# Two chunks of the state-space recurrence per visit, norm sums as columns, one operand for two running sums

## The chip, the core and the metric

The kernel runs on one core of one Trainium2 chip. The engines that matter are PE (TensorE, the matmuls), DVE (VectorE), ACT (ScalarE), POOL (GpSimd, which does elementwise work here) and SP (SyncE, which issues most DMAs). Each engine takes its own instructions strictly in the order in which they stand in its queue, and semaphores order the engines among each other. The metric is the device time of one execution in microseconds (us); lower is better.

## What is computed

One decoder layer over 1024 tokens of width 1024, all in float32. One projection of the normalized input gives all branches; a state-space branch (Mamba-2, chunked) and an attention branch with a forget gate are gated, merged, projected and normalized. The part that the change touches:

```python
dt = softplus(dt_raw + dt_bias);  a = -exp(a_log)
da_cs = cumsum(dt * a)                       # within each chunk of 128 tokens, per head
decay = exp(where(causal, da_cs[l] - da_cs[s], -inf))
y_diag = (C B^T * decay) @ (xs * dt)         # within the chunk
states = B^T @ (xs * dt * exp(da_cs[-1] - da_cs))
# over the chunks, one after the other:
carry = carry * exp(da_cs[-1]) + states
y_off = (C @ carry_before) * exp(da_cs)
y = y_diag + y_off + xs * d_skip
# gated group norm: 4 groups of 256 channels
yg = y * silu(z_ssm);  yg = yg * rsqrt(mean(yg * yg) + eps) * g
# attention: F = cumsum(log_sigmoid(f)) over all tokens, per head
```

There are 16 heads of 64 channels in 4 groups; a group shares B and C (128 states).

## The kernel before

**The stream.** All large products go through PE as one long list of steps. A step is one of the seven products of a fast matrix multiplication for a pair of weight columns; it is 12 matmuls of 128 x 512 (each operand is split into a high and a low part), in two halves of six. `Stream.half()` issues the next half. The other work of the kernel is written as generators: `stream.beside(gen)` runs a piece of such a generator and then as many halves as it yields. On PE everything stands in program order (`mm`, `turn`), so PE's order is what this weaving makes of it. ACT and DVE prepare the weights of the steps ahead (tiles `wop`, `sum`) and take the results out of PSUM (`s`, `th`, `u`). On ACT, DVE and POOL only the instructions in `pin` keep program order among themselves; the others are put where a scheduler finds a place by its own estimate of time, and `tc.high_priority()` moves an instruction ahead of others that could start. Once built, the order on each engine is fixed.

**The recurrence.** `ssd(g)` does one group of four heads, chunk by chunk (8 chunks of 128 tokens). Of a chunk there are:
- `sums(c)`: a DMA by SP that spreads the running sums of the chunk over all partitions (tile `csb`, three chunks ahead);
- `decays(c)`: on ACT four Relu and one Exp make the decay matrix `m4`;
- `first(c)`: on PE the turns (transposes) of two value tiles and of B, and the product of B and C (all into PSUM tile `tr`); DVE makes `xdt` and `cbm` from them and multiplies `m4` by `cbm`; ACT copies the turned B to `bn`;
- `more(c)`: on POOL `xe` (the weighted values for the state), on ACT `ce = Exp(csb)`, on POOL `ce` times C;
- `second(c)`: on PE the state product (`st`), on POOL the old state times its decay (`new`), on DVE that plus `st`; on PE the outputs into `yps`, first `m4` by `xdt` (within the chunk), then `ce` by the state before (carried in); after each second chunk DVE adds the skip path.

One visit of a chunk issues `first(c + 1)`, then `second(c)`, then `more(c + 1)`; four halves of the stream lie between one visit and the next. So the state that `second(c)` makes is used one visit later, and what `first` and `more` prepare is used one visit later.

**Norm sums.** `squares(g, ch, ...)` adds the squares of 256 channels per token: the squares are split in a high and a low part (ACT, DVE), two matmuls of 128 x 512 against a matrix of ones give the sums in all rows (`pv`), ACT copies one row, and four one-row turns make columns of it (`pv_t`).

**Running sums.** `dt_and_f()` makes `dtn` (dt and log f side by side) and `da = -dt * a`; three products of `da` (`pt_te`) give the sums after a token, of the chunk and up to a token, as columns; four products per half of the tokens give the sums as rows (`pt_cs`), and four more those of log f (`pt_f`).

Buffers of the pool `sp`: `csb` 2, `ce` 1, `xe` 1, `bn` 1, `m4` 2, `xdt` 2.

Of the kernel before, what the change touches and what calls it, by code (L numbers as in the profile page):

```python
# [86 lines left out]
def hybrid_layer(ctx: ExitStack, tc, a, out):  # L87
# [596 lines left out]
    def dt_and_f():  # L684

        def rows(tag, bufs):
            t = sp.tile([P, 4, P], F32, tag=tag, bufs=bufs, name="rows")
            return t.rearrange("p a b -> p (a b)")[0:HEADS, :]

        pair = [  # L690
            sp.tile([P, 4, P], F32, tag="csb", bufs=2, name="t").rearrange("p a b -> p (a b)") for _ in range(2)
# [24 lines left out]
        for n in (13, 11, 9, 7, 5, 3, 1):  # L716
# [7 lines left out]
        nc.vector.scalar_tensor_tensor(  # L724
            dtn[:, :, 0:16], w[:, :, 0:16], 2.0, z2[:, :, 0:16], ALU.mult, ALU.add
        )
        nc.vector.scalar_tensor_tensor(
            dtn[:, :, 16:32], w[:, :, 16:32], -2.0, z2[:, :, 16:32], ALU.mult, ALU.add
        )

        nc.vector.scalar_tensor_tensor(
            da, dtn[:, :, 0:16], -1.0, ea.unsqueeze(1).to_broadcast([P, NT, HEADS]), ALU.mult, ALU.mult
        )
        yield 8

        daf = da.rearrange("p c h -> p (c h)")
# [4 lines left out]
        nc.scalar.activation(tend, pe_[:, 0:P].rearrange("p (c h) -> p c h", c=NT), AF.Exp)  # L741
        nc.scalar.activation(cdec, pe_[:, P : 2 * P].rearrange("p (c h) -> p c h", c=NT), AF.Exp)
        nc.scalar.activation(cscol, pe_[:, 2 * P : 3 * P].rearrange("p (c h) -> p c h", c=NT), AF.Copy)
# [10 lines left out]
        fc = [rows("ce", 1), rows("csb", 2)]  # L754
        for ch in range(2):
            pf = pp.tile([P, HALF], F32, tag="tr", bufs=2, name="pt_f")
            for j in range(4):
                c = ch * 4 + j
                mm(
                    pf[0:HEADS, j * P : (j + 1) * P], dtn[:, c, 16:32], tri, start=True, stop=True  # L760
                )
            for j in range(4):
                c = ch * 4 + j
                o, w = fc[ch][:, j * P : (j + 1) * P], pf[0:HEADS, j * P : (j + 1) * P]
# [76 lines left out]
    def ssd(g):  # L841
# [4 lines left out]
        def sums(c):  # L846

            if c < NT:
                csb = at[c]["csb"] = sp.tile([P, 4, P], F32, tag="csb", bufs=2, name="csb")
                nc.sync.dma_start(csb, cs_dram[hs, c * P : (c + 1) * P].unsqueeze(0).to_broadcast([P, 4, P]))  # L850

        def first(c):
# [16 lines left out]
            if c < NT - 1:  # L869
                bn = s["bn"] = sp.tile([P, P], F32, tag="bn", bufs=1, name="bn")  # L870
# [17 lines left out]
        def more(c):  # L888
# [3 lines left out]
            if c < NT - 1:  # L892
                xe = s["xe"] = sp.tile([P, 4, 64], F32, tag="xe", bufs=1, name="xe")
# [5 lines left out]
            if c > 0:  # L899
                ce = s["ce"] = sp.tile([P, 4, P], F32, tag="ce", bufs=1, name="ce")  # L900
                tc.keep_in_program_order(nc.scalar.activation(ce, s["csb"], AF.Exp))
                pin(nc.gpsimd.tensor_tensor(ce, ce, ct[:, cs].unsqueeze(1).to_broadcast([P, 4, P]), ALU.mult))

        def second(c, prev, yps):

            s = at[c]
            new = None
            if c < NT - 1:
                st = pp.tile([P, 4, 64], F32, tag="st", bufs=1, name="st")
                mm(st, s["bn"], s["xe"], start=True, stop=True)  # L910
                new = sp.tile([P, 4, 64], F32, tag="prev", bufs=3, name="new")
# [897 lines left out]
```

## Time and profile before

| | |
|---|---|
| time, median of 3 runs | 1274.74 us (1272.76 to 1275.68) |
| profiled execution, from its first to its last instruction | 1276.3 us (1.6 above the median of the runs) |
| PE busy | 1247.9 us, 98% |
| DVE busy | 1015.9 us, 80% |
| ACT busy | 793.9 us, 62% |
| POOL busy | 320.7 us, 25% |

The profile gives no time of that execution apart from its span. Up to about 20 us the inputs arrive; the projection with the recurrence of the four groups beside it lies from there to about 690 us (the groups' recurrences at about 132 to 196, 287 to 353, 424 to 488 and 559 to 623 us); then comes attention, and the last products end at 1276 us.

A row of the timeline is: start in us, length in us, engine, line, operation, written tile <- read tiles, shape, number of instructions taken together, and in brackets the idle time before it with what ended it. Matmuls overlap, so the time that one takes of PE is the distance between two starts, not its length; a product of plain float32 operands is two instructions there. Instructions of ACT, DVE and POOL overlap a little as well. A row of the groups is: line, engine, operation, tiles, shape, count | busy us in all, mean ns of one | idle us before them.

### The profile page before, as it was taken

The numbers are of one execution on the slowest core, as the hardware profiler recorded it, in microseconds if no ns is written. First come the engines' busy times: TensorE is split into PE (matmuls) and PEld (weight loads), VectorE is DVE, ScalarE is ACT, GpSimd is POOL, SyncE is SP. The second block draws the span as 40 slices with busy tenths as digits, with TensorE's granted clock in tenths as the row PEclk, the third lists the DMA queues.
The fourth block names the chain that finished last, engine by engine and source line by source line (L and its number), as shares of the span: only waits on it lengthen the run. The fifth ranks groups of instructions, "written<-read, shape, count | busy, mean of one in ns | idle before, by whom it ended". The sixth has DMA issues, their size and how long they took to land.

```text
span 1276.3 us, 20821 instructions
## 1 busy us (share of the span) xinstructions
PE 1247.9 (98%) x6926; PEld 984.3 (77%) x6926; DVE 1015.9 (80%) x1996; ACT 793.9 (62%) x1735; POOL 320.7 (25%) x322
## 2 busy tenths in 40 slices
PE   5999999999999999999999999999999999999997
PEld 4688878787888888888887777777777777778886
DVE  7988896888888978997767676767789767797975
ACT  7745665556665665566555666666687666743753
POOL 4000350013400241114102123223112212356052
PEclk9999999999999999999999999999999999999999
DMA  8232452645437533644447476666688657666932
GB/s 295 70 122 74 142 167 89 186 151 185 125 108 222 166 120 128 214 141 141 148 144 251 160 232 214 215 217 214 232 282 278 209 193 252 234 203 214 367 113 102
DMA packets 152235, 233.56 MB, mean 183 GB/s; under 512 B 15200, under 2 KB 60736, under 8 KB 152128
## 3 DMA queue, kind: packets, MB, share of 16 engines
q1 hardware_dynamic: 136064, 196.08, 48.0%
q10 hardware_dynamic: 10560, 18.06, 3.7%
q0 software_dynamic: 5504, 18.09, 3.7%
q8 instruction: 54, 0.88, 0.3%
q14 instruction: 53, 0.43, 0.1%
HBM read 162.99 MB, written 72.34 MB: 184 GB/s over the span
## 4 chain that ended last, share of the span: by engine, by line
PE 73%; DMA 9%; DVE 8%; ACT 4%; issue 4%; SPq 1%; POOL 1%; DVEq 0%; ACTq 0%; POOLq 0%
PE pb L128 30%; PE pc L128 18%; PE pd L128 6%; PE pt L131 4%; PE av L128 4%; PE s L128 4%; PE yps L128 2%; DVE wop L351 2%; ACT ex L1525 1%; DMA xt<-in_x 1%; DMA raw<-in_wu 1%; PE st L128 1%; DVE sum L356 1%; PE tr L131 1%; PE tr_v L131 1%
## 5 line engine op out<-in xcount | busy, mean ns | idle before, releaser
L350 ACT ACTIVATE wop<-sum 128x512 fp32r<-128x512 f32 x180 | 112.7, 627 | 112.7 <-DVE sum L356 50.0
L351 DVE TENSOR_TENSOR wop<-sum,wop 128x512 fp32r<-128x512 f32 x180 | 138.4, 771 | 52.0 <-ACT wop L350 50.9
L1525 ACT ACTIVATE ex<-ex,nm 128x512 f32<-128x512 f32 (+1 forms) x192 | 116.3, 607 | 74.0 <-DVE nm L1521 73.6
L410 ACT ACTIVATE s<-pb 128x512 f32<-128x512 f32 x143 | 84.8, 593 | 92.9 <-PE pb L128 90.6
L128 PE MATMUL pb<-x0h,wop 128*128 128x512 f32 x384 | 132.0, 400 | 0.0
L128 PE MATMUL pc<-x3h,wop 128*128 128x512 f32 x384 | 129.8, 395 | 1.3 <-DVE th L423 0.9
L128 PE MATMUL pc<-x2h,wop 128*128 128x512 f32 x384 | 130.3, 398 | 0.4 <-DVE u L425 0.4
L351 DVE TENSOR_TENSOR wop<-raw,wop 128x512 fp32r<-128x512 f32 x144 | 107.1, 745 | 29.5 <-ACT wop L350 28.1
L128 PE MATMUL pb<-x4h,wop 128*128 128x512 f32 x384 | 129.2, 395 | 0.0
L128 PE MATMUL pb<-x6h,wop 128*128 128x512 f32 x376 | 127.3, 396 | 1.3 <-ACT s L410 1.3
L128 PE MATMUL pb<-x5h,wop 128*128 128x512 f32 x376 | 127.3, 395 | 0.4 <-ACT s L410 0.4
L1521 DVE CUSTOM_DVE_ANT_0 ex<-s,fb 128x512 f32<-128x512 f32 (+1 forms) x192 | 96.8, 552 | 21.0 <-PE s L128 15.2
L350 ACT ACTIVATE wop<-raw 128x512 fp32r<-128x512 f32 x144 | 89.8, 624 | 14.6 <-PE pd L128 5.9
L128 PE MATMUL pd<-x1h,wop 128*128 128x512 f32 x288 | 96.3, 394 | 0.0
L128 PEld LDWEIGHTS pb<-x0h,wop 128*128 128x128 f32 x384 | 72.8, 190 | 17.6 <-issue 2.9
L128 PEld LDWEIGHTS pc<-x3h,wop 128*128 128x128 f32 x384 | 72.1, 188 | 18.5 <-issue 1.5
L128 PEld LDWEIGHTS pc<-x2h,wop 128*128 128x128 f32 x384 | 72.1, 188 | 17.9 <-issue 2.4
L128 PEld LDWEIGHTS pb<-x6h,wop 128*128 128x128 f32 x376 | 71.0, 189 | 18.5 <-issue 2.2
L128 PEld LDWEIGHTS pb<-x4h,wop 128*128 128x128 f32 x384 | 72.1, 188 | 16.7 <-issue 1.9
L211 POOL TENSOR_TENSOR wd<-wd 128x256 f32<-128x256 f32 x32 | 33.0, 1033 | 202.8 <-DMA wd<-in_wo 122.0
L128 PEld LDWEIGHTS pb<-x5h,wop 128*128 128x128 f32 x376 | 70.6, 188 | 17.3 <-issue 2.0
L895 POOL TENSOR_TENSOR xe<-xdt,tend 128x256 f32<-128x256 f32 x28 | 26.1, 932 | 201.2 <-DVE xdt L863 196.9
(328 smaller groups left out, 3058.8 us busy)
## 6 DMA issues: line engine op xcount, KB each, us to landing
raw<-in_wu SPq DMA_DIRECT2D x128, 256.0 KB
csb<-cs_dram SPq DMA_DIRECT2D x32, 256.0 KB
q<-q_dram SPq DMA_DIRECT2D x32, 256.0 KB
k<-k_dram SPq DMA_DIRECT2D x16, 512.0 KB
fb<-f_dram SPq DMA_DIRECT2D x16, 512.0 KB
rb<-st_dram SPq DMA_DIRECT2D x48, 128.0 KB
wd<-in_wo SPq DMA_DIRECT2D x40, 128.0 KB
xt<-in_x SPq DMA_DIRECT2D x8, 512.0 KB
```

The source lines that it names most:

```text
L128: return tc.keep_in_program_order(nc.tensor.matmul(*args, **kw))
L131: return tc.keep_in_program_order(nc.tensor.transpose(out_, in_, idn))
L211: pin(nc.gpsimd.tensor_tensor(t[out_], t[a_], t[b_], ALU.subtract))
L350: nc.scalar.activation(op[:, 0], src, AF.Copy)
L351: nc.vector.tensor_tensor(op[:, 1], src, op[:, 0], ALU.subtract)
L356: self.adds.tensor_tensor(t, x, y, ALU.add)
L410: nc.scalar.activation(s, ps, AF.Copy)
L895: nc.gpsimd.tensor_tensor(xe, s["xdt"], tend[:, c, hs].unsqueeze(2).to_broadcast([P, 4, 64]), ALU.mult)
L1521: nc.vector.tensor_tensor_reduce(o, s[e][:, 0:w], fb[hp, h][:, e, 0:w], 1.0, 3.0e38, ALU.add, ALU.min, nm)
L1525: pin(nc.scalar.activation(o, o, AF.Exp, scale=-1.0, bias=nm, accum_out=hd.at(hd.sm, i, h, e)))
```

## The change

In words:
- `ssd(g)` goes over pairs of chunks (a, b). One visit issues `first(a)`, `first(b)`, then `more(a)`, `more(b)`. Four halves later a second visit issues, on PE: the state product of a, the outputs of a within and carried, the outputs of b within, those of b carried (which need the state after a), and the state product of b. Then come four halves with `decays` of the next pair. There are still eight halves to two chunks; the lead-in of a group is shorter by four halves, and these come later in the stream.
- The addition that ends a state on DVE gets high priority. `ce` is now written over `csb`, which has three buffers; `xe` and `bn` have two. The first output of a pair clears the whole PSUM bank (`start`), the others accumulate.
- The turns of the value tiles for attention (`tr_v`) get more places at which they can be issued.
- The norm sums are made as columns at once: four products of a 128 x 128 block of squares with one column of ones. The split of the squares, the copy of the row and its turns are gone.
- The operands of both running sums lie in one tile (`both_sums`: 16 columns of `da`, 16 of zero, 16 of log f), so one product of 48 rows gives both. The sum after a token is now the chunk's sum less the sum up to it (DVE), instead of a product with `stri`; `stri` and `da` are gone.

**PE, second group, chunks 2 and 3.** Before, one visit to chunk 2 (with `first` of chunk 3) stands between two steps like this:

```order
L131 MATMUL tr<-ident,xs_2595 128x128
L131 MATMUL tr<-ident,xs_2705 128x128
L131 MATMUL tr<-ident,bt 128x128
L128 MATMUL tr<-ct,bt 128x128
L128 MATMUL st<-xe,bn 128x256
L128 MATMUL yps<-m_2975,xdt 64x128 x2
L128 MATMUL yps<-ce,new 64x128 x2
L131 MATMUL tr_v<-ident,th 128x128 x4
```

Now the turns of both chunks stand alone, 24 matmuls of the stream and a `tr_v` follow, and then this stands between two steps:

```order
L128 MATMUL st<-xe,bn 128x256
L128 MATMUL yps<-m_2971,xdt 64x128 x4
L128 MATMUL yps<-csb,new 64x128 x4
L128 MATMUL yps<-m_3002,xdt 64x128 x4
L128 MATMUL yps<-csb,new 64x128 x4
L128 MATMUL st<-xe,bn 128x256
```

The two state products frame the outputs of both chunks, and the last group of outputs reads the state that the first row begins.

**ACT, the same place.** `s` takes a step's result out of PSUM, `wop` and `wl` prepare weights, `th<-tr_v` copies a turned value tile. Before, for chunk 3 alone:

```order
L882 ACTIVATE m4_3069<-csb_2943,cscol_640 128x128 x4
L350 ACTIVATE wop_3075<-raw_2748 128x512
L886 ACTIVATE m4_3069<-m4_3069 128x512
L350 ACTIVATE wop_3137<-sum_2891 128x512
L871 ACTIVATE bn_3106<-tr_3097 128x128
L901 ACTIVATE ce_3124<-csb_2943 128x512
L833 ACTIVATE th_3134<-tr_v_3129 128x512
```

Now, for chunks 2 and 3 (`csb_2766` and `csb_2937`):

```order
L410 ACTIVATE s_3056<-pb_2862 128x512
L240 ACTIVATE wl_3058<-wd_1247 128x256
L350 ACTIVATE wop_3069<-raw_2720 128x512
L826 ACTIVATE th_3066<-tr_v_3061 128x512
L864 ACTIVATE bn_3029<-tr_3020 128x128
L894 ACTIVATE csb_2766<-csb_2766 128x512
L894 ACTIVATE csb_2937<-csb_2937 128x512
```

Both exponentials of the running sums stand behind the copy `s` of the step that lies on PE right behind the turns (the first of two before the second visit), behind three more instructions of the stream's, and behind the copy of the second chunk's B.

**POOL, the same place.** Before:

```order
L895 TENSOR_TENSOR xe_3033<-xdt_3011,tend_638 128x256
L902 TENSOR_TENSOR ce_3035<-ce_3035,ct_2369 128x512
L916 TENSOR_TENSOR new_3111<-new_3020,cdec_639 128x256
L895 TENSOR_TENSOR xe_3122<-xdt_3102,tend_638 128x256
L902 TENSOR_TENSOR ce_3124<-ce_3124,ct_2369 128x512
L916 TENSOR_TENSOR new_3196<-new_3111,cdec_639 128x256
```

Now:

```order
L888 TENSOR_TENSOR xe_3032<-xdt_3013,tend_637 128x256
L895 TENSOR_TENSOR csb_2766<-csb_2766,ct_2341 128x512
L888 TENSOR_TENSOR xe_3036<-xdt_3025,tend_637 128x256
L895 TENSOR_TENSOR csb_2937<-csb_2937,ct_2341 128x512
L909 TENSOR_TENSOR new_3093<-new_2932,cdec_638 128x256
L909 TENSOR_TENSOR new_3114<-new_3093,cdec_638 128x256
```

The decayed state of the first chunk (`new_3093`) now stands behind both chunks' other products.

**ACT, second group, chunks 0 and 1.** Behind the turns of both chunks there now stands:

```order
L410 ACTIVATE s_2875<-pb_2862 128x512
L875 ACTIVATE m4_2823<-csb_2764,cscol_639 128x128 x4
L350 ACTIVATE wop_2889<-sum_2887 128x512
L826 ACTIVATE th_2882<-tr_v_2877 128x512
L879 ACTIVATE m4_2823<-m4_2823 128x512
L864 ACTIVATE bn_2850<-tr_2841 128x128
L894 ACTIVATE csb_2764<-csb_2764 128x512
```

The exponential for chunk 1 (`csb_2764`), which had a visit of its own, stands behind the copy `s` of the first step after the turns and five more lines.

The core of the diff:

```diff
     def dt_and_f():
...
+        nc.vector.scalar_tensor_tensor(dtn, w[:, :, 0:16], 2.0, z2[:, :, 0:16], ALU.mult, ALU.add)
+        for n, t in enumerate(both_sums):
+            own = slice(4 * n, 4 * n + 4)
+            nc.vector.memset(t[:, :, 16:32], 0.0)
+
+            nc.vector.scalar_tensor_tensor(
+                t[:, :, 0:16], dtn[:, own, :], -1.0, ea.unsqueeze(1).to_broadcast([P, 4, HEADS]), ALU.mult, ALU.mult
+            )
+            nc.vector.scalar_tensor_tensor(
+                t[:, :, 32:48], w[:, own, 16:32], -2.0, z2[:, own, 16:32], ALU.mult, ALU.add
+            )
         yield 8
-        mm(pe_[:, 0:P], stri, daf, start=True, stop=True)
-        mm(pe_[:, P : 2 * P], ones, daf, start=True, stop=True)
-        mm(pe_[:, 2 * P : 3 * P], tri, daf, start=True, stop=True)
...
+        for n, t in enumerate(both_sums):
+            mm(pe_[:, 64 * n : 64 * n + 64], ones, t[:, :, 0:16], start=True, stop=True)
+            mm(pe_[:, P + 64 * n : P + 64 * n + 64], tri, t[:, :, 0:16], start=True, stop=True)
...
-                mm(pc[0:HEADS, j * P : (j + 1) * P], da[:, ch * 4 + j, :], tri, start=True, stop=True)
+                mm(pc[0:48, j * P : (j + 1) * P], both_sums[ch][:, j, 0:48], tri, start=True, stop=True)
...
             if c > 0:
-                ce = s["ce"] = sp.tile([P, 4, P], F32, tag="ce", bufs=1, name="ce")
-                tc.keep_in_program_order(nc.scalar.activation(ce, s["csb"], AF.Exp))
+                ce = s["ce"] = s["csb"]
+                pin(nc.scalar.activation(ce, ce, AF.Exp))
                 pin(nc.gpsimd.tensor_tensor(ce, ce, ct[:, cs].unsqueeze(1).to_broadcast([P, 4, P]), ALU.mult))
...
+                with tc.high_priority():
                     nc.vector.tensor_tensor(new, new, st, ALU.add)
+            return new
...
+        for c in range(3):
+            sums(c)
         yield 2
         decays(0)
         yield 2
-        first(0)
-        more(0)
-        sums(2)
         decays(1)
-        yield 4
-        for c in range(NT):
...
+        for a in range(0, NT, 2):
+            b = a + 1
+            with tc.high_priority():
+                first(a)
+                first(b)
+            if early:
                 next(early, None)
+            more(a)
+            more(b)
+            yield 2
+            turn_values()
+            yield 2
+            yps = pp.tile([P, 2, 2 * P], F32, tag="y", bufs=1, name="yps")
+            mid = state(a, prev)
+            within(a, yps)
+            if a:
+                carried(a, prev, yps)
+            within(b, yps)
+            carried(b, mid, yps)
+            prev = state(b, mid)
+            skipped(b, yps)
+            sums(a + 3)
+            sums(a + 4)
...
             turn_values()
             yield 2
-            decays(c + 2)
+            decays(a + 2)
+            turn_values()
             yield 2
+            decays(b + 2)
...
-        nc.scalar.activation(sqp[0], zs[0], AF.Copy)
-        nc.vector.tensor_tensor(sqp[1], zs[0], sqp[0], ALU.subtract)
         yield 6
-        pv = pp.tile([P, HALF], F32, tag="tr", bufs=2, name="pv")
-        for j in range(2):
-            mm(pv, onesr, sqp[j], start=(j == 0), stop=(j == 1))
-        nc.scalar.activation(line, pv[0:1, :], AF.Copy)
-        yield 2
...
         for b in range(4):
-            turn(pc[:, b : b + 1], line[:, b * P : (b + 1) * P], ident[0:1, 0:1])
+            mm(pc[:, b : b + 1], zs[0][:, b * P : (b + 1) * P], ones[:, 0:1], start=True, stop=True)
```

More of the change, by code (lines that the diff above doesn't have):

```diff
@@ L944, in ssd @@
         yield 2
[L945 to L947 removed]
         decays(1)
[L949 to L966 removed]
+        for a in range(0, NT, 2):
[4 more added lines that the diff above has]
+            if early:
+                next(early, None)
+            more(a)
[14 more added lines that the diff above has]
+            sums(a + 4)
+            if early:
+                next(early, None)
+            if a == 2:
+                z = sp.tile([P, T + 4], F32, tag="u", bufs=2, name="z")
+                early = squares(g, 0, [z[:, half(j)] for j in range(2)])
                 next(early)
@@ L1004, in flat @@
             return sp.tile([P, 4, P], F32, tag=tag, bufs=bufs, name=name).rearrange("p a b -> p (a b)")
-        yield from squares(
-            g, 1, [flat("csb", 2, "z") for _ in range(2)], [flat("m4", 2, "sqp").bitcast(F32R) for _ in range(2)],
-            flat("ce", 1, "line")[0:1],
-        )
+        yield from squares(g, 1, [flat("csb", 3, "z") for _ in range(2)])
         rc = groups[g]["rc"]
@@ L1301, in hybrid_layer @@
     ) as pp:
[L1302 to L1303 removed]
+        ones = sp.tile([P, P], F32, name="ones")
         nc.vector.memset(ones, 1.0)
```

142 lines of the change are left out of this document (60 added, 82 removed).

## The prediction

> **What bounds the kernel now.** First the page's row of busy times:
>
> ```profile
> PE 1247.9 (98%) x6926; PEld 984.3 (77%) x6926; DVE 1015.9 (80%) x1996; ACT 793.9 (62%) x1735; POOL 320.7 (25%) x322
> ```
>
> PE is the bound. Then the busy time in the stretch of the fourth group's recurrence (columns: stretch, length, then PE, PEld, DVE, ACT and POOL with their instructions, the granted clock, DMA), and PE's waits, in which the stage has one entry:
>
> ```profile
> 559.00:623.00 64.00, 64.00 (x394) 51.56 (x392) 52.23 (x89) 41.94 (x96) 24.28 (x24) 1.00 0.50 157
> ...
> PE yps L128 <- DVE m L873: 0.7, 1, 0.7
> ```
>
> PE is busy for 64.00 of 64.00 us at full clock. So each us that the change takes from PE's list is a us of the kernel, and so is each us that PE is made to wait. Last, PE's timeline over one visit of a chunk:
>
> ```profile
> 319.50 0.38 PE L131 MATMUL tr<-ident,xs 128*128 128x128 f32 x2
> 319.72 0.27 PE L131 MATMUL tr<-ident,bt 128*128 128x128 f32 x1
> 319.83 0.39 PE L128 MATMUL tr<-ct,bt 128*128 128x128 f32 x2
> 320.05 0.60 PE L128 MATMUL st<-xe,bn 128*128 128x256 f32 x2
> 320.58 0.44 PE L128 MATMUL yps<-m,xdt 128*64 128x128 f32 x4
> 320.85 0.39 PE L128 MATMUL yps<-ce,new 128*64 128x128 f32 x4
> 321.07 0.39 PE L128 MATMUL yps<-m,xdt 128*64 128x128 f32 x4
> 321.29 0.39 PE L128 MATMUL yps<-ce,new 128*64 128x128 f32 x4
> 321.61 0.66 PE L131 MATMUL tr_v<-ident,th 128*128 128x128 f32 x4
> 322.02 0.48 PE L128 MATMUL pb<-x6h,wop 128*128 128x512 f32 x1
> 322.33 0.40 PE L128 MATMUL pb<-x6l,wop 128*128 128x512 f32 x1
> ```
>
> The distances between starts count. A 128-column instruction takes 0.11 (319.72 to 319.83), the five of the turns 0.55 with nothing lost; a group of four outputs 0.22 (321.07 to 321.29). The state product is two instructions of 256 columns, 0.45 at that rate; `tr_v` is four, 0.45. That makes 0.55 + 0.45 + 0.88 + 0.45 = 2.33. The visit takes 2.52, and the first stream matmul behind it 0.31 where two others take 0.46 (369.73 to 370.19 below is of that shape): 2.60. So 0.27 goes to the passage from 128-column to 64-column products and back; the gaps behind `st` and behind the last `yps` show it.
>
> **What the change takes from PE.** Outputs are visited 32 times before (8 chunks, 4 groups) and 16 times after: 16 x 0.27 = **4.3** (3.2 to 5.3, if the passage is 0.2 or 0.33). The turns alone cost no passage, nor does `tr_v` alone.
>
> Running sums and norm sums, before, with the only product here that moves 64 columns (`pt_df`):
>
> ```profile
> 59.75 1.10 PE L128 MATMUL pt_df<-summing,dft 128*128 128x64 f32 x8 [0.55 <-DVE summing L1320]
> 60.66 0.48 PE L128 MATMUL pc<-x2h,wop 128*128 128x512 f32 x1
> ...
> 85.26 0.39 PE L128 MATMUL pt_te<-da,stri 128*128 128x128 f32 x2
> ...
> 87.00 0.50 PE L128 MATMUL pc<-x3h,wop 128*128 128x512 f32 x1
> ...
> 89.64 0.39 PE L128 MATMUL pc<-x3h,wop 128*128 128x512 f32 x1
> ...
> 90.93 0.50 PE L128 MATMUL pb<-x5h,wop 128*128 128x512 f32 x1
> ...
> 369.73 0.62 PE L128 MATMUL pv<-sqp,onesr 128*128 128x512 f32 x2
> 370.19 0.39 PE L128 MATMUL pb<-x6h,wop 128*128 128x512 f32 x1
> ...
> 373.03 0.40 PE L131 MATMUL pv_t<-ident,line 1*128 1x1 f32 x4
> 373.36 0.50 PE L128 MATMUL pc<-x2h,wop 128*128 128x512 f32 x1
> ```
>
> The first piece of the running sums takes 1.74 (85.26 to 87.00), the three others 1.06 each (89.64 + 0.23 to 90.93): 4.92. After, the first piece has eight 64-column instructions, which took 0.91 for `pt_df`, and four products of rows at 1.06; the second 1.06: 3.03. Gain **1.9**.
>
> A norm sum takes 0.46 + 0.33 and some 0.09 of entry, 0.88. Four products against one column are eight instructions; the rows show that a short one is not cheaper than 0.11 (`pt_df`: 64 columns, 0.91 for eight). So 0.9 after: **0**. If one column cost half as much, 8 x 0.45 = 3.6 more would be gained. The copies and the split that go (ACT and DVE) lie beside PE and count nothing.
>
> With the old wait of 0.7 that makes **6.9** (5 to 11).
>
> **What it adds: waits of PE for its own pair.** The last outputs of a pair need the state after its first chunk, whose product starts the same visit, and `ce` of both chunks. Before, all these had a visit's time. Now 24 matmuls (5.5 us, with `tr_v` 6.0) lie between the turns and the visit, and ACT, POOL and DVE have both chunks to do in them. Rows that price it (timelines of ACT and POOL, groups of POOL and DVE):
>
> ```profile
> 586.83 0.60 ACT L410 ACTIVATE s<-pb 128x512 f32<-128x512 f32 x1 [2.17 <-PE pb L128]
> 587.33 1.27 ACT L882 ACTIVATE m<-csb,cscol 128x128 f32<-128x128 f32 x4
> 588.50 0.62 ACT L350 ACTIVATE wop<-raw 128x512 fp32r<-128x512 f32 x1
> 589.02 0.41 ACT L237 ACTIVATE wl<-wd 128x256 fp32r<-128x256 f32 x1
> 589.33 0.62 ACT L886 ACTIVATE m<-m 128x512 f32<-128x512 f32 x1
> 589.85 0.58 ACT L410 ACTIVATE s<-pb 128x512 f32<-128x512 f32 x1
> ...
> 590.85 0.26 ACT L871 ACTIVATE bn<-tr 128x128 f32<-128x128 f32 x1
> 591.64 0.63 ACT L901 ACTIVATE ce<-csb 128x512 f32<-128x512 f32 x1 [0.53 <-PE yps L128]
> ...
> 584.25 1.76 POOL L902 TENSOR_TENSOR ce<-ce,ct 128x512 f32<-128x512 f32 x1 [0.55 <-ACT ce L901]
> 585.97 0.61 POOL L916 TENSOR_TENSOR new<-new,cdec 128x256 f32<-128x256 f32 x1
> ...
> 592.35 1.29 POOL L902 TENSOR_TENSOR ce<-ce,ct 128x512 f32<-128x512 f32 x1 [1.05 <-ACT ce L901]
> ...
> L902 POOL TENSOR_TENSOR ce<-ce,ct 128x512 f32<-128x512 f32 x28 | 41.8, 1494 | 36.4 <-ACT ce L901 36.3
> L895 POOL TENSOR_TENSOR xe<-xdt,tend 128x256 f32<-128x256 f32 x28 | 26.1, 932 | 201.2 <-DVE xdt L863 196.9 <-PE yps L128 4.3
> ...
> L920 DVE TENSOR_TENSOR new<-new,st 128x256 f32<-128x256 f32 x24 | 9.9, 412 | 0.0
> ```
>
> On ACT, from start to start: `s` 0.50, decays 1.17, `wop` 0.52, `wl` 0.31, Exp of `m4` 0.52; `bn` 0.26, `ce` 0.63 to its end; for the copy of `tr_v` I take 0.50, as for `s`. A handover from engine to engine is 0.08 (`ce` ends at 592.27, POOL starts at 592.35). A matmul's result comes 0.16 behind its turn on PE (0.39 long, 0.23 apart).
>
> *Chunks 2 and 3 of a group.* By the new order on ACT both `ce` stand behind `s` of the step right behind the turns. From that step's end: 0.16 + `s` 0.50 + `wl` 0.31 + `wop` 0.52 + copy 0.50 + `bn` 0.26 + `ce` 0.63 = 2.88. Then POOL, in its order: `ce` 1.49, `xe` 0.93, the other `ce` 1.49, `new` 0.93 (as `xe`, same shape): 4.84. DVE's addition 0.41, three handovers 0.24: the state stands 8.4 behind that step. PE from the same point: `tr_v` 0.45, a step of 12 x 0.23 = 2.76, `st` 0.53, the outputs ahead 0.27 + 5 x 0.22: 5.11. PE would wait 3.3. With POOL at its short rows (1.29, 0.61) it is 2.2, with `ce` at 1.76 3.8. I take 2.8, between the short rows and the means, since DVE, beside whose work POOL is slow, has its products with `m4` done by then. Four groups: **11.2** (9 to 15). POOL's `wd` slips in before `new` in the first and fourth group, another us each, which I leave to the range.
>
> *Chunks 0 and 1.* There is no `new` on POOL, but `ce` of chunk 1 stands behind `s` of the first step, the decays, `wop`, copy, Exp, `bn`: 0.16 + 0.50 + 1.17 + 0.52 + 0.50 + 0.52 + 0.26 + 0.63 = 4.26, POOL 1.49, handovers 0.16: 5.9. PE: 0.45 + 2.76 + 0.53 + 0.49 + 0.44 = 4.67. Wait 1.2 (0 if ACT ran ahead, 1.5 with POOL at 1.76); the groups differ a little, I take 1.1: **4.5**.
>
> *Chunks 4 to 7.* There the two `ce` stand ahead of the stream's copies on ACT, and the decays of both chunks have run before the turns. POOL is done before the visit: **0** (up to 1.2 each by DVE's queue, below).
>
> Behind a waiting PE the whole stream stands. Behind DVE's waiting addition stand the skip path and the `wop` of steps some three ahead, which PE does not need within 3 us. On SP the `csb` loads now wait until PE has read the old buffer, with weight loads behind them; the third buffer and two steps of lead hide that (0; a late weight load would show as DVE idle before `sum`).
>
> [...]
>
> **Sum.** 1276.3 - 6.9 + 11.2 + 4.5 = 1285.1 for a profiled execution. That of before lies 1.6 above the median of the runs, so **1284**; its own range is 1278 to 1289.
>
> **Rivals.**
> *The waits are hidden; faster.* If ACT and POOL run ahead of PE as they do now, so that the state stands within 5.1 of the step, only the gain is left: 1276.3 - 6.9 - 1.6 = 1268. For it: PE's one wait in these stages, and ACT idle for a third of them. Against: the fixed order on ACT, which begins at a PE step, and POOL's four products behind it.
> *DVE's queue decides; slower still.* The high priority only places the addition; DVE must reach it. The row of `new<-new,st` has no idle time before 24 of them: it always came out of a queue. In one chunk:
>
> ```profile
> 303.18 0.60 PE L128 MATMUL st<-xe,bn 128*128 128x256 f32 x2
> ...
> 308.83 0.41 DVE L920 TENSOR_TENSOR new<-new,st 128x256 f32<-128x256 f32 x1
> ```
>
> The addition starts 5.05 behind the product's end (303.78). From there PE has 1.3 until it needs the state; the addition and two handovers take 0.57 of them, so it may start 0.7 late. At 1.9 late, under half of that row, in the eight visits that I gave no wait, that is 8 x 1.2 = 9.6 more: 1294. Against: the DVE has lighter work between the pairs and catches up.
> *Both cancel; no change.* With waits in chunks 2 and 3 alone and POOL short, 9 against 6.9 to 11: 1272 to 1277. It decides where `ce` gets ahead of the copies.
>
> **How the numbers follow.** The forecast 0.43, DVE's queue 0.20, cancelled 0.10, hidden 0.27. A measurement tells 0.2% (2.5 us) from no change; so slower 0.63, same 0.10, faster 0.27. The range for 8 in 10 reaches from a little under the hidden case, 1265, to the DVE case, 1294.
>
> **What would show it.** Right: PE idle before `yps`, released by DVE `new` or POOL `ce`, some 12 us over the eight first two visits of the groups, and none in the fourth pair; PE's busy time down by 6 to 7; visits of both outputs with one gap behind `st`. Wrong: no entry of `yps` in PE's waits and a span near 1269; or waits in all sixteen visits, released by DVE after a run of `wop` and `sum`; or norm sums under 0.5 us on PE.

## The result and the profile after

The changed kernel takes 1311.77 us (median of 5 runs, 1306.91 to 1316.44), the kernel before 1274.74 us (5 runs, 1272.76 to 1275.7). The ratio is 1.0288, with a 95% interval of 1.0271 to 1.0305: slower by 37 us, where 9 were forecast and the range ended at 1294.

The rows that answer those of the forecast: busy times and granted clock over 40 slices (the profile's page), the stretch of the fourth group's recurrence (length, PE, PEld, DVE, ACT, POOL, clock, DMA), and PE's waits ahead of the outputs (us in all, times, longest).

```profile
PE 1259.9 (96%) x6928; PEld 997.1 (76%) x6928; DVE 1022.4 (78%) x1993; ACT 787.4 (60%) x1719; POOL 320.4 (24%) x321
...
PEclk9999989999999989999999999999999999999999
...
584.00:664.00 80.00, 74.30 (x425) 60.16 (x425) 61.28 (x103) 46.19 (x107) 27.84 (x24) 0.96 0.41 128
...
PE yps L128 <- DVE new L914: 19.6, 10, 3.8
...
PE yps L128 <- POOL csb L895: 5.0, 7, 2.0
...
PE yps L128 <- DVE m L866: 0.4, 2, 0.2
```

Two things are new. PE waits 24.6 us ahead of the outputs, for the state of its own pair and for `ce` (here named `csb`). And PE is busy for longer, 1259.9 us instead of 1247.9, though it has less to do: in the recurrence the granted clock is no longer 1.00.

The longest kind of wait, chunks 2 and 3 of the first group: PE, then POOL, then DVE (timelines).

```profile
157.51 0.66 PE L128 MATMUL yps<-m,xdt 128*64 128x128 f32 x8
161.81 0.66 PE L128 MATMUL yps<-csb,new 128*64 128x128 f32 x8 [3.64 <-DVE new L914]
162.40 1.22 PE L128 MATMUL st<-xe,bn 128*128 128x256 f32 x2
163.06 0.99 PE L128 MATMUL pb<-x5h,wop 128*128 128x512 f32 x1
...
155.46 1.45 POOL L895 TENSOR_TENSOR csb<-csb,ct 128x512 f32<-128x512 f32 x1 [4.52 <-ACT csb L894]
156.87 1.06 POOL L888 TENSOR_TENSOR xe<-xdt,tend 128x256 f32<-128x256 f32 x1
157.90 1.71 POOL L895 TENSOR_TENSOR csb<-csb,ct 128x512 f32<-128x512 f32 x1
159.56 1.17 POOL L211 TENSOR_TENSOR wd<-wd 128x256 f32<-128x256 f32 x1
160.69 0.61 POOL L909 TENSOR_TENSOR new<-new,cdec 128x256 f32<-128x256 f32 x1
...
161.33 0.42 DVE L914 TENSOR_TENSOR new<-new,st 128x256 f32<-128x256 f32 x1 [1.19 <-POOL new L909]
```

This is the chain of the forecast: `ce`, `xe`, `ce`, a `wd` that slips in, `new`, each on POOL's heels, then the addition on DVE, then PE. Behind the wait the state product takes 1.22 us where it took 0.60 (320.05 in the forecast's visit), and the stream's matmul 0.99 instead of 0.40.

That is the clock. All 17 changes of the granted clock in this trace lie whole multiples of 3.41 us from one another (those at 162.34, 165.75, 182.81 and 189.64 are 1, 5 and 2 apart). The same stretch cut at these multiples, called windows from here on (columns as above: length, PE, PEld, DVE, ACT, POOL, granted clock):

```profile
155.51:158.92 3.41, 2.47 (x28) 1.47 (x26) 3.38 (x4) 0.91 (x2) 3.41 (x3) 1.00 0.40 137
158.92:162.34 3.42, 0.53 (x8) 0.42 (x8) 1.65 (x2) 0.00 (x0) 2.89 (x4) 1.00 0.48 113
162.34:165.75 3.41, 3.41 (x12) 2.69 (x9) 2.86 (x5) 0.61 (x2) 0.84 (x2) 0.50 0.35 91
165.75:169.16 3.41, 3.41 (x17) 2.81 (x16) 1.77 (x3) 2.10 (x5) 0.00 (x0) 1.00 0.14 22
...
179.40:182.81 3.41, 0.41 (x8) 0.41 (x8) 3.41 (x7) 1.64 (x5) 0.91 (x2) 1.00 0.53 170
182.81:186.23 3.42, 3.42 (x17) 2.89 (x14) 1.61 (x6) 0.80 (x2) 0.61 (x1) 0.50 1.03 340
186.23:189.64 3.41, 3.41 (x9) 2.64 (x8) 0.69 (x1) 0.00 (x0) 0.00 (x0) 0.50 0.68 256
189.64:193.05 3.41, 3.41 (x16) 2.77 (x15) 1.36 (x2) 0.63 (x1) 0.00 (x0) 1.00 0.00 0
```

A window in which PE did 0.53 us of work is followed by one at half clock; after a window of 0.41 us there are two. In a window at half clock the stream's matmuls start 0.42 to 0.43 apart (163.85 to 165.55), behind it 0.23 (166.34 to 167.71); the loss is put at half of each such window, 1.7 us. Before attention there are nine of them, none before the change.

The whole, counted in both timelines up to the start of the stream's 2441st matmul (just ahead of attention) and from there on. Idle time and half clock are counted from 60 us on; the start, with its wait for the inputs, is in the rest:

| us | before | after | difference |
|---|---|---|---|
| PE idle in the visits of the recurrence | 0.7 | 25.3 | +24.5 |
| PE idle elsewhere in the stretch | 1.7 | 1.5 | -0.2 |
| lost to half clock (half the length of the windows) | 0 | 15.4 | +15.4 |
| the rest: the start, and PE's own work at full clock | 681.4 | 676.9 | -4.5 |
| start of that matmul | 683.9 | 719.0 | +35.2 |
| from there to the end | 592.5 | 595.7 | +3.2 |
| span | 1276.3 | 1314.7 | +38.4 |

The last 3.2 us lie in attention, which the change doesn't touch. In the kernels below that part takes 590.2 to 594.6 us; it was not followed up.

### The profile page after: what moved, and what is told of

Read it like the earlier page. It is cut to its first block, busy times and chain, and to the rows that moved or that the text cites. A ratio compares the mean times of both kernels' runs of the same rounds, so it can differ in the third digit from the quotient of the medians.

```text
span 1314.7 us, 20757 instructions
## 1 busy us (share of the span) xinstructions
PE 1259.9 (96%) x6928; PEld 997.1 (76%) x6928; DVE 1022.4 (78%) x1993; ACT 787.4 (60%) x1719; POOL 320.4 (24%) x321
## 4 chain that ended last, share of the span: by engine, by line
PE 40%; DVE 5%; DMA 5%; ACT 3%; issue 2%; POOL 1%; SPq 0%; DVEq 0%; ACTq 0%; POOLq 0%
PE pb L128 15%; PE pc L128 10%; PE av L128 4%; PE s L128 4%; PE pt L131 4%; PE pd L128 2%; DVE wop L351 1%; DMA xr<-in_x 1%; DMA x3l<-t_s 1%; ACT ex L1534 1%; DMA raw<-in_wbs 1%; DMA x4l<-t_w 1%; ACT wop L350 0%; DMA th<-gs_dram 0%; ACT m L875 0%
## 5 line engine op out<-in xcount | busy, mean ns | idle before, releaser
L351 DVE TENSOR_TENSOR wop<-sum,wop 128x512 fp32r<-128x512 f32 x180 | 144.4, 803 | 48.9 <-ACT wop L350 48.0
L128 PE MATMUL pb<-x5h,wop 128*128 128x512 f32 x376 | 132.0, 409 | 0.5 <-ACT s L410 0.5
L1530 DVE CUSTOM_DVE_ANT_0 ex<-s,fb 128x512 f32<-128x512 f32 (+1 forms) x192 | 96.8, 552 | 19.6 <-PE s L128 14.4
L350 ACT ACTIVATE wop<-raw 128x512 fp32r<-128x512 f32 x144 | 89.7, 624 | 34.7 <-PE pd L128 24.6
L128 PEld LDWEIGHTS pb<-x5h,wop 128*128 128x128 f32 x376 | 73.3, 195 | 18.1 <-issue 1.8
```

Source lines behind the costliest of these rows:

```text
L128: return tc.keep_in_program_order(nc.tensor.matmul(*args, **kw))
L350: nc.scalar.activation(op[:, 0], src, AF.Copy)
L351: nc.vector.tensor_tensor(op[:, 1], src, op[:, 0], ALU.subtract)
L1530: nc.vector.tensor_tensor_reduce(o, s[e][:, 0:w], fb[hp, h][:, e, 0:w], 1.0, 3.0e38, ALU.add, ALU.min, nm)
```

## The experiments

Theory: PE waits for its own pair (ACT, POOL and DVE have 24 matmuls of time for work that had a visit's), and the half clock follows from these waits. Rivals: the new sums share in the loss; the half clock is not paid; DVE's queue alone makes the state late. Each kernel is compared with the kernel before on the same chip. Waits, half clock and rest are counted as in the table above. These three columns are of the one profiled execution, which can lie some us off the median: 1316.4 for the changed kernel (the slowest of its five), 1304.9 for `half_filled`, 1293.2 for `ready_lead`.

| kernel | us | ratio (95% interval) | PE idle in visits | half clock | rest |
|---|---|---|---|---|---|
| before | | 1 | 0.7 | 0 | 681.4 |
| changed | 1311.8 | 1.0288 (1.0271 to 1.0305) | 25.3 | 15.4 | 676.9 |
| no_pairs | 1272.8 | 0.9967 (0.9953 to 0.998) | 0 | 0 | 677.8 |
| filled | 1297.8 | 1.017 (1.0147 to 1.0193) | 12.4 | 0 | 693.1 |
| half_filled | 1301.7 | 1.0207 (1.0186 to 1.0229) | 18.2 | 8.5 | 685.1 |
| new_first | 1290.5 | 1.0121 (1.01 to 1.0141) | 15.9 | 1.7 | 678.3 |
| decays_sooner | 1297.6 | 1.0176 (1.016 to 1.0193) | 19.6 | 6.8 | 677.9 |
| early_ce | 1314.1 | 1.0295 (1.0271 to 1.0319) | 29.8 | 10.2 | 678.8 |
| all_ready | 1297.5 | 1.0177 (1.0154 to 1.0199) | 19.2 | 6.8 | 676.7 |
| ready_lead | 1288.7 | 1.0093 (1.0072 to 1.0114) | 13.9 | 5.1 | 677.1 |
| step_between | 1296.1 | 1.0148 (1.012 to 1.0177) | 13.8 | 5.1 | 682.0 |
| old_state | 1300.4 | 1.019 (1.0166 to 1.0214) | 20.7 | 8.5 | 678.0 |
| paired_outputs | 1268.9 | 0.9948 (0.9929 to 0.9968) | 2.4 | 1.7 | 672.2 |
| paired_sooner | 1272.5 | 0.9974 (0.9964 to 0.9984) | 4.2 | 0 | 674.8 |

Between kernels with the same work on PE (the changed one, and new_first, decays_sooner, early_ce, all_ready, ready_lead and old_state, which move things on the other engines) the rest differs by 2 us, while waits and half clock together go from 18 to 41. So these two carry the differences; one or two us of the rest say nothing.

**no_pairs: the sums without the pairs.** `ssd` of before, with the new `dt_and_f` and `squares`:

```diff
-        for a in range(0, NT, 2):        # pairs, as changed
...
+        for c in range(NT):              # chunk by chunk, as before
+            ...
+            prev = second(c, prev, yps)
```

> The recurrence of before, chunk by chunk, with the new running sums and norm sums. Theory (the whole loss is the pairing's): 1274.7 less the 1.9 us of the running sums, norm sums the same: 1271 to 1274, no waits before yps over 1 us, the granted clock as before (0.998). Rival (the sums have a share in the loss, by their waits or by what they do to the order on ACT and DVE): over 1278.

Measured 1272.8, no wait ahead of `yps`. The loss is the pairing's, and the sums are a gain. The rest falls by 3.6 us.

**filled and half_filled: useless work where PE waited.**

```diff
             within(b, yps)
+            if a == 2 or (g == 0 and a == 4):
+                spare = pp.tile([P, HALF], F32, tag="tr", bufs=2, name="spare")
+                for n in range(24):      # half_filled: range(12)
+                    turn(spare[:, n % 4 * P : n % 4 * P + P], ident)
             carried(b, mid, yps)
```

> The changed kernel with 24 turns of the unit matrix, whose results nobody reads (2.6 us of PE), ahead of the last outputs of chunks 2 and 3 in all groups and of chunks 4 and 5 in the first, so that PE works where it waited longest. Theory (the clock is halved behind a long wait, and that is paid): the five waits shrink by 2.6 each and PE's busy time grows by as much, so the visits stay as long, but the half clock behind them (1.7 + 3.4 + 1.7 + 3.4 + 1.7 = 11.9 us lost) goes: 1300 (1297 to 1303). Rival (the half clock is only recorded, or comes from something else): 1312, or some us more.

Measured 1297.8, 14 us less than the changed kernel, with 13 us more of work. The same place as above (PE's timeline):

```profile
157.89 2.84 PE L131 MATMUL spare<-ident 128*128 128x128 f32 x24
161.62 0.66 PE L128 MATMUL yps<-csb,new 128*64 128x128 f32 x8 [0.89 <-DVE new L914]
162.21 0.70 PE L128 MATMUL st<-xe,bn 128*128 128x256 f32 x2
162.55 0.58 PE L128 MATMUL pb<-x5h,wop 128*128 128x512 f32 x1
```

The last outputs begin at 161.62 instead of 161.81, so the visit is no shorter; but the state product takes 0.70 instead of 1.22 and the stream goes on at full clock. All nine windows of half clock went. Seven of them lay behind the filled places: these were caused by PE's idle time, and they are paid. Of the two others, one lay behind a stop of the stream at 414 us that this run doesn't have, and one behind a wait of 0.87 us that it has as well; why the second went is open.

> The changed kernel with 12 useless turns (1.3 us) instead of 24 in the five places where PE waited longest. The visits stay as long, the five waits come to 2.3, 2.5, 1.3, 1.3 and 1.9 us. If a window of 3.41 us is halved when the one before it held more than about 1.9 us of idle time, as in all windows so far, and below that only now and then, two or three of the seven windows of half clock stay (the two long waits, and where the rest shares a window with an earlier wait): 1300 to 1306. Rival (any wait over 1 us halves the clock): six or seven stay, 1308 to 1312.

Measured 1301.7, in the range, but with five half windows in the recurrence instead of two or three. One of them is new, behind the wait of chunks 0 and 1 of the first group, which no filling touched (windows of 3.41 us of this kernel, then of the changed one):

```profile
140.29:143.71 3.42, 1.42 (x15) 1.07 (x12) 3.39 (x4) 0.95 (x2) 2.91 (x3) 1.00 0.15 55
143.71:147.12 3.41, 3.41 (x9) 2.65 (x9) 1.45 (x4) 0.00 (x0) 0.81 (x1) 0.50 0.51 173
```

```profile
138.44:141.86 3.42, 1.97 (x20) 1.22 (x19) 3.38 (x7) 2.32 (x5) 1.06 (x1) 1.00 0.49 153
141.86:145.27 3.41, 2.86 (x18) 2.33 (x19) 3.30 (x5) 0.00 (x0) 2.65 (x3) 1.00 0.32 115
```

It is the same wait of 2.00 us at 140.4. In one run it lies whole in a window, in the other a boundary at 141.86 cuts it in two, and the clock stays. So the price of this wait hung on where the windows fell: one at half clock behind it in one run, none in the other.

**new_first: one instruction of POOL moved ahead.** The product of the state before the pair with its decay is issued ahead of `more(a)`:

```diff
+            mid = decayed(a, prev)       # new = prev * cdec, on POOL
             more(a)
             more(b)
...
-            mid = state(a, prev)
+            mid = state(a, prev, mid)    # only st and the addition
```

> The changed kernel with POOL's product of the old state with its decay for the first chunk of a pair put ahead of xe and ce of both chunks, where it stood behind them. Theory (POOL's queue of ce, xe, ce, new makes the state late): in chunks 2 and 3 the outputs could go on when ce of the second chunk is made, 2.1 us sooner in the first and fourth group, 1.0 in the others; the waits come to 18, and with the idle time per window under 1.9 us there three to five windows of half clock go (5 to 8 us): 1298 to 1302. Rival (POOL's whole work between the turns and the outputs counts, whatever its order): ce and xe come as much later, the wait only moves: 1308 to 1314.

Measured 1290.5, below the range of the theory. PE's waits:

```profile
PE yps L128 <- POOL csb L895: 10.7, 10, 2.0
...
PE yps L128 <- DVE new L922: 3.6, 5, 1.1
```

What DVE's addition ended fell from 19.6 to 3.6 us; most of what is left is `ce`. The waits fell by 9.4 us, where 6.5 were expected, and the half clock by 13.7, to one window, where 5 to 8 were expected: most of the surplus is the clock. The waits fell by more because the addition moved too: in chunks 4 and 5 of the first group it had stood in DVE's queue until 181.94, although POOL was done at 179.93 (178.87 + 1.06), behind two `th`, a `sum` and a `wl`; with its operand early it got a place 1.1 us behind the state product, and that wait fell from 3.81 to 0.33.

**decays_sooner: ACT's decays two halves ahead.**

```diff
+            decays(a + 2)
             turn_values()
             yield 2
-            decays(a + 2)
+            decays(b + 2)
             turn_values()
             yield 2
-            decays(b + 2)
```

> The changed kernel with the decays of both chunks of the next pair two halves sooner (the first right behind the outputs, the second two halves before the turns instead of at them). Theory (ACT's list behind the turns, with the second chunk's decays in it, makes ce late): chunks 2 and 3 win up to 1.7 us each and chunks 4 to 7 something; waits 24.5 to 17, some windows of half clock go: 1297 to 1304. Rival (the decays are off the path, or now stand ahead of the stream's copies and make these late): no gain, 1308 to 1316, the waits under other names.

Measured 1297.6, as the theory had it: ACT's list behind the turns is a part of the chain. The waits fell less than expected (to 19.6 instead of 17), the half clock from nine windows to four.

**early_ce: both `ce` right behind the decays.** The two lines of `ce` move from `more(c)` to the end of `decays(c)`.

> The changed kernel with both ce operations (Exp on ACT, the product with C on POOL) made right behind the decays of their chunk, up to four halves ahead of the turns, instead of behind the turns. Theory (the two ce on ACT and POOL ahead of the decayed state are what makes the state late): waits before yps fall from 24.5 to 3 to 8 us, half clock to 2 or less: 1276 to 1284. Rival (DVE's queue holds the addition): waits stay over 12 us, DVE busy with wop and sum ahead of the addition, 1293 or more.

Measured 1314.1: no gain, a miss. The waits ahead of the outputs did fall, to 7.8 us, but the rest of the wait went to the state product ahead of them (PE's waits; then POOL and PE, chunks 0 and 1 of the second group):

```profile
PE st L128 <- POOL xe L896: 21.9, 13, 3.6
...
308.39 1.58 POOL L884 TENSOR_TENSOR csb<-csb,ct 128x512 f32<-128x512 f32 x1 [18.09 <-ACT csb L882]
309.94 2.08 POOL L896 TENSOR_TENSOR xe<-xdt,tend 128x256 f32<-128x256 f32 x2
...
311.05 1.10 PE L128 MATMUL st<-xe,bn 128*128 128x256 f32 x2 [3.37 <-POOL xe L896]
```

The second chunk's decays are issued just ahead of the turns, so its `ce` came no sooner; but on POOL it now stood ahead of both `xe`, and those are needed first. The new order only moved the wait.

**all_ready and ready_lead: all three together.** `new_first`, `decays_sooner` and `early_ce` in one; `ready_lead` with `yield 2` more between `decays(1)` and the first turns of a group.

> The changed kernel with all of it: decays two halves sooner, both ce operations with them, and the product of the old state ahead of xe. Between the turns and the outputs ACT has only bn, POOL only xe for both chunks and the old state. Theory (ACT's and POOL's work of the pair between the turns and the outputs is what PE waits for): waits 3 us or less, no half clock in the recurrence, the gains of 6.9 left: 1268 to 1276. Rival (DVE's queue holds xdt, the products with the decays or the addition): waits of about 10, 1280 to 1292.

Measured 1297.5, a miss, above both ranges. In chunks 2 to 7 the waits fell to 5.4 us; most of what is left stands at the starts of the groups, as do four of these five waits (11.7 us):

```profile
PE st L128 <- POOL xe L896: 13.6, 5, 3.8
```

> The changed kernel with decays and ce two halves sooner and the old state's product first, and with two halves more between the decays of chunk 1 and the first turns of a group. Theory (of the 18.6 us of waits left without these two halves, 13.6 were for xe of the first chunk behind ce of the second on POOL, which stands behind the decays on ACT at the start of a group): these 13.6 shrink to 3 or less and the 6.8 us of half clock behind them go: 1275 to 1282. Rival (the start of a group is late for another reason, its conv and gate work on ACT and DVE, which moves with it): 1290 or more.

Measured 1288.7, between the ranges of theory and rival. These 13.6 us fell to 2.3, as expected, but others grew: from 1.4 to 3.3 us ahead of `tr_v` for ACT's `bn`, from 4.0 to 6.4 ahead of the outputs for states. Each repair showed the next queue.

**step_between: a step of the stream inside the visit.**

```diff
             within(b, yps)
+            yield 2
+            decays(a + 2)
             carried(b, mid, yps)
...
-            turn_values()
-            yield 2
-            decays(a + 2)
```

> The changed kernel with one step (12 matmuls, 2.7 us) of the four ahead of a pair's turns moved between the outputs of b within the chunk and those carried. Theory (PE waits for the state of its own pair, and the half clock follows from these waits): 24.5 us of waits become 3 or less, 15.4 us of half clock become 1.7 or less, 16 more passages to 64 columns cost 4.3: 1276 to 1282. Rival (what delays the state is a queue that the stream itself lengthens, so the state comes as much later as the outputs): waits of over 12 us stay, 1295 or more.

Measured 1296.1, the rival's number, but not its reason. The wait for the state is nearly gone, but in its place PE waits for `ce` and for the products with the decays, in chunks 0 to 3:

```profile
PE yps L128 <- POOL csb L895: 6.8, 3, 2.9
...
PE yps L128 <- DVE m L866: 3.0, 5, 1.5
...
PE yps L128 <- DVE new L914: 1.5, 2, 0.8
```

The step came from the time ahead of the turns, and ACT and POOL probably lacked it there; no run tried that alone. In the second to fourth group, chunks 4 to 7 have no wait ahead of their outputs.

**old_state: the dependence on the own pair's state left out.**

```diff
-            carried(b, mid, yps)
+            carried(b, prev if a else mid, yps)
```

> The changed kernel whose outputs of the second chunk, from chunk 3 on, are carried from the state before the pair instead of the state after its first chunk, so that part of the computation is left out and PE needn't wait for the state of its own pair there. Theory (the state is last): the 19.6 us of waits that DVE's addition ended shrink to those for ce, 8 to 12 us in all, one or two windows of half clock stay: 1285 to 1292. Rival (ce comes just before the state everywhere, so that the state adds little): waits over 18, 1300 or more.

Measured 1300.4, a miss and the rival's number: the wait for the addition did not go with the dependence (PE's waits).

```profile
PE yps L128 <- POOL csb L895: 10.4, 12, 2.0
...
PE st L128 <- DVE new L914: 7.9, 6, 2.9
```

The state product of the second chunk needs the one PSUM buffer `st`, which the same addition has to read first. So a late addition stops the visit twice, and this run could not part the two.

**paired_outputs: the passages saved without the wait.** Turns, state product and state go chunk by chunk, as before; only the outputs stand together, in the odd chunk's visit, and read the state of a visit earlier. The even chunk's product with its decays is issued behind the outputs, and the addition has no priority here:

```diff
+            after[c] = state(c, after[c - 1])
+            if c % 2 == 1:
+                yps = pp.tile([P, 2, 2 * P], F32, tag="y", bufs=1, name="yps")
+                for d in (c - 1, c):
+                    within(d, yps)
+                    if d:
+                        carried(d, after[d - 1], yps)
```

> Outputs in pairs without a wait for the own pair: turns, state product and state chunk by chunk as before, 24 matmuls apart; only the outputs of two chunks stand in one visit, that of the odd chunk, and read the state made a visit earlier. With the new running sums and norm sums; ce over csb (three buffers), xdt three buffers, xe and bn one. Theory (what costs is the need of the own pair's state and ce within one gap of the stream, and the 16 passages saved are worth 0.27 each): the 1272.8 of the kernel chunk by chunk with the new sums, less 4.3, no wait before yps over 1 us, no half clock: 1267 to 1271. Rival (the passages saved are worth nothing, or the decays, now made later, wait for csb and bring waits of their own): 1273 or more, PE waiting for the products with the decays on DVE.

Measured 1268.9, faster than both kernels. PE's timeline over a visit of the second group, and the stretch of that group:

```profile
316.78 0.60 PE L128 MATMUL st<-xe,bn 128*128 128x256 f32 x2
317.31 0.66 PE L128 MATMUL yps<-m,xdt 128*64 128x128 f32 x8
...
318.67 0.61 PE L128 MATMUL yps<-csb,new 128*64 128x128 f32 x8
...
296.00:370.00 74.00, 74.00 (x447) 61.62 (x446) 56.98 (x98) 47.20 (x98) 24.56 (x24) 1.00 0.45 136
```

PE is busy for 74.00 of 74.00 us at full clock, with one passage for two chunks. One wait is left, 2.4 us in the first group, for a product with the decays on DVE.

> Outputs in pairs without a wait for the own pair, and the decays of the odd chunk two halves sooner (two halves behind the visit with the outputs instead of just ahead of the next). The one wait that the version without this has (2.4 us in the first group, for the second chunk's product with its decays, and 1.7 us of half clock behind it) should go if those decays were late on ACT: 1264 to 1267. Rival (ACT then waits for the running sums that have just been asked for, and holds up the stream's copies): 1268 or more, with waits under other names.

With `decays(c + 2)` moved between two `yield 2`, measured 1272.5: the rival's number. The wait in the first group fell from 2.4 to 0.3 us, and two of 1.7 came, in the second and third group:

```profile
PE yps L128 <- DVE m L869: 3.7, 3, 1.7
```

Waits and half clock together stay as they were (4.2 against 4.1 us); the loss lies in the rest, and its cause is open.

## Why the prediction was wrong in size

The direction held, and PE waits for its own pair, as forecast. But the forecast of 1284 was 28 us short, and the time lies outside the range. The step that failed is the price of a wait: it was put at its length, and the half clock that follows, 15.4 us, stood in no term. For the profiled execution 1285.1 was forecast and 1314.7 measured. Of these 29.6 us the half clock is 15.4, the waits are 9.5 more than forecast, the gains 1.7 less, attention is 3.2, and other idle time -0.2.

- **"Waits of PE for its own pair", 15.7 us: 24.6 in the waits.** By place (sum of the four groups): chunks 0 and 1 were put at 4.5, and PE's timeline has 3.4; chunks 2 and 3 at 11.2, and it has 13.7; chunks 4 to 7 at nothing, and it has 7.5. For chunks 2 and 3 the chain gave 3.3 a group, "I take 2.8"; measured are 3.4. In all four groups DVE was idle there until POOL was done, and the addition started 0.03 behind it. POOL had its long rows (1.06 for `xe`, 1.71 for `ce`, and a `wd` in the first group), and the reason given for the discount, DVE's lighter work, did not hold. For chunks 4 to 7 it was DVE's queue: in all six visits with a wait the addition started 1.1 to 2.0 us after both its operands were there, behind work for the stream. In five of the six that is more than PE waited. Chunks 4 and 5 of the second group, where PE waited 0.46 us (POOL, then DVE):

```profile
342.88 1.06 POOL L909 TENSOR_TENSOR new<-new,cdec 128x256 f32<-128x256 f32 x1
...
344.52 0.69 DVE L356 TENSOR_TENSOR sum<-raw 128x512 f32<-128x512 f32 x1
345.13 0.68 DVE L427 TENSOR_TENSOR th<-s,pc 128x512 f32<-128x512 f32 x1
345.73 0.41 DVE L914 TENSOR_TENSOR new<-new,st 128x256 f32<-128x256 f32 x1
```

  Of the signs named, PE's waits came as said, but with 17 us in the first two visits of the groups instead of 12, and 1.9 in the fourth pair instead of none; PE's busy time went up by 12 instead of down by 6 to 7, since PE counts as busy all through a window at half clock, where its matmuls start 0.42 to 0.43 apart instead of 0.23.
- **POOL's long rows.** The second `ce` of chunks 2 and 3 took 1.70 to 1.71 in all four groups, where the forecast took the mean of 1.49. That POOL is slow beside DVE's work shows in a part of its rows only. In the changed kernel `new` took 0.61 in the eight places where DVE was idle and 0.99 to 1.06 in the sixteen others; but `xe` of the same shape took 0.61 to 0.62 in sixteen of 28 places, with DVE busy for 73% or more of each, and two of those four `ce` took 1.71 with DVE busy for 0.59 of it. DVE's `sum`, of the shape of `ce`, took 0.64 to 0.69 in the 105 places where POOL was idle and 0.67 to 1.80 in the 51 others.
- **"So is each us that PE is made to wait": this step failed.** It put the price of a wait at its length. Measured: another 15.4 us went to the half clock, 13.7 of them behind the 24.5 us of waits, and `filled` shows for seven of the nine windows that it is the idle time that brings them. No term of the sum, no rival and no bound had it. A trace of the kernel before did hold it, in one place of attention (windows of 3.41 us):

```profile
1107.91:1111.32 3.41, 2.38 (x22) 1.74 (x24) 1.32 (x3) 3.41 (x9) 2.73 (x3) 1.00 0.74 234
1111.32:1114.74 3.42, 3.42 (x17) 2.17 (x14) 3.38 (x12) 1.54 (x6) 0.76 (x2) 0.50 0.15 56
```

- In the changed kernel windows with 0.17 us (from 612.89) to 2.55 us of PE's work in them (from 633.37) were followed by half clock.
- **"Gains, 6.9".** Of these, 0.7 is the old wait. Of the other 6.2 the rest shows 4.5. The sums gave 3.6 (`no_pairs`) where 1.9 were expected: the running sums gave 1.9 (how far the 300th matmul of the stream came nearer to the 100th), which leaves 1.7 for the eight norm sums and whatever else moved with them, instead of nothing. That a short product is hardly cheaper held: it was put at 0.11, and the eight of `pv` below take 0.81 (494.23 to 495.04), 0.10 each.

```profile
492.04 0.61 PE L128 MATMUL yps<-m,xdt 128*64 128x128 f32 x8
493.11 0.66 PE L128 MATMUL yps<-csb,new 128*64 128x128 f32 x8 [0.46 <-DVE new L914]
493.69 0.70 PE L128 MATMUL st<-xe,bn 128*128 128x256 f32 x2
494.23 0.95 PE L128 MATMUL pv<-ones,z 128*128 128x1 f32 x8
495.04 0.64 PE L131 MATMUL tr_v<-ident,th 128*128 128x128 f32 x4
```

- The passages, 4.3 by the forecast, show only 0.9 (677.8 to 676.9) in the changed kernel, less than the 2 us by which the rest scatters. The same rows say part of why: eight outputs take PE 0.45 (three such groups from 317.31 to 318.67 in `paired_outputs`), so behind those at 492.04 the next could begin at 492.49; they begin at 493.11, 0.62 later, and the row calls 0.46 of that idle. A stop costs 0.16 more than the idle time in the trace; over some 16 stops that is 2.6, an estimate from this one visit. `paired_outputs`, which has no such stops but one, gets 5.6 of rest (677.8 to 672.2), where 4.3 were expected.
- **"SP and csb loads: 0".** The sign named for a late weight load did come once, at 414 us: DVE idle for 4.7 us ahead of `sum`, PE 1.5 us idle behind it and one window at half clock (1.7 of the 15.4). In the other kernels of the table this stop is 0 to 1.1 us; no run tried its cause.
- **The rivals.** That DVE's queue decides in all sixteen visits is not so: in chunks 2 and 3 DVE waited for POOL, and `new_first`, which moves one instruction of POOL's, takes 16 us from what the addition ends. In chunks 4 to 7 it did decide: the rival had 9.6 us in eight visits, measured are 7.5 in six, and that DVE "catches up" between the pairs did not hold. The hidden case is not this kernel's. `paired_outputs` comes to its number (1268 against 1268.9) partly by luck: its rest gains 9.2 instead of 6.2, and a wait with the half clock behind it (4.1 us) takes that surplus back.

## What to carry to other kernels

Price a wait of the bounding engine by the clock as well as by its length (here 15.4 us of half clock beside 25.3 of idle time): look in the trace of before for the granted clock behind the waits that are there, and add that to the sum. Before work is gathered in fewer visits, ask what each part needs from its own visit; put together only those parts whose inputs are a visit old, as `paired_outputs` does. The late chain here, over ACT, POOL and DVE, had several queues in it, and freeing one showed the next; the cheapest repair here was to issue first, on the fullest queue, what had its inputs first.

## What the hardware showed

The half clock came in windows of 3.41 us: in the changed kernel they begin at 162.34, 182.81 and 329.59, 6 and 43 times 3.41 apart, and no change of the granted clock in its trace lies between two such multiples. Over the fourteen profiled executions (windows at full clock from 25 us on, up to 7 us before the end, by the idle PE time in them): with 0.3 to 0.85 us idle none of 170 was followed by half clock, with 0.85 to 1.4 five of 74, with 1.4 to 1.9 fourteen of 31, above 1.9 all of 28 but one, which held 1.90. In the traces of before and of the changed kernel alone these are none of 27, three of 8, one of 2 and all of 5. What decides between 0.85 and 1.9 us is open, and so is why some windows of half clock are followed by a second.
